# A gated retention and sparse attention block: the first stage's buffers, chunk order and queues

## The chip, the cores and the metric

The kernel runs on one core of one Trainium2 chip. The metric is the device time of one execution in microseconds; lower is better. The runs of the kernel before have a median of 1617.08 us (three runs, 1615.84 to 1619.18).

## The reference

One decoder block over 512 positions and 2048 channels, all in 32-bit floats. An adaptive norm makes h; fifteen projections of h, held in one matrix w_in, feed a retention branch and a sparse attention branch (NSA); both are gated, widened and merged, and one output projection closes the block.

```python
mod = silu(c) @ w_ada + b_ada                 # 2048 -> 3 * 2048
shift, scl, gate = split(mod, 3)
h = rmsnorm(x, g_norm) * (1 + scl) + shift
(r_q, r_k, r_v, r_g, n_q, n_kc, n_vc, n_ks, n_vs, n_kw, n_vw, n_g, n_bg, m_a, m_b) = split(h @ w_in)
y_ret = retention(rope(r_q), rope(r_k), r_v) * silu(r_g)
y_nsa = nsa(rope(n_q), n_kc, n_vc, rope(n_ks), n_vs, rope(n_kw), n_vw, sigmoid(n_bg)) * silu(n_g)
merged = sigmoid(m_a) * (y_ret @ w_up_ret) + sigmoid(m_b) * (y_nsa @ w_up_nsa)
x = x + gate * (merged @ w_out)
out = rmsnorm(x, g_final)
```

## The kernel before

Every large product is made of three matmuls with reduced-precision parts: activation and weight are split into a high part (a cast by ScalarE, `whi`, `hhi`) and a low part (a subtraction by VectorE, `wlo`, `hlo`), and TensorE adds high x high, high x low and low x high into a PSUM bank. Weights come in tiles of 128 x 1024 (512 KB). `plan` lists all of them in order of use; `load` runs ahead of use and issues the transfers on SP's queue while buffers are free; `split` makes the two parts of the next weight tile, three of them at most being held. The schedule is that of the program text: each engine executes its instructions in the order in which they are written.

The first stage makes h and, beside it, the first two groups of w_in (`g0`, the compressed keys and values; group 1, the keys `kT`). The modulation is computed in 8 chunks of 256 channels of shift and scale. A chunk is 8 tiles of w_ada. `ada_batch` takes two of them and runs 4 matmuls, four at a time on the four column quarters of the array (`pa`). After four batches `ada_rows` copies the sums out, `ada_cols` turns them into columns with small matmuls (`misc`), and VectorE and ScalarE make the high and low parts of two 128-channel tiles of h. `xn` multiplies x by the norm's scale first. Between batches TensorE works off a queue `todo` of steps of group 0 (one weight tile, one of four banks, 6 matmuls) and of group 1 (`k_step`: a tile with half the columns and four contraction tiles, 12 matmuls, in one of two banks; the sum is added to `kacc` by VectorE). A step carries the number of the batch from which it may run, and each batch lets about 12 matmuls go.

Buffers of the stage: 5 tiles (`raw`) and 2 pairs (`kv`), 9 tiles in all. The norm's sum of squares is 16 matmuls with a matrix of ones; `rstd_rows` turns it into the scale `rstd` after the second batch. The rotary tables are built one VectorE instruction per batch; the last `k_step`s rotate the keys. Then groups 2 to 20 follow in `run_group`, with `side` items (attention, retention) put in by `tick` at a `rate` for each step. Later stages that the change touches: the up-projections reload gates (`sg`) from memory on SP's queue, and the output's evacuation sums squares and scales the rows.

## Time and profile before

| | |
|---|---|
| median of the runs | 1617.08 us |
| profiled execution, its own time | 1619.62 us |
| its span | 1617.9 us |
| TensorE busy | 1588.0 us (98%) |
| VectorE, ScalarE busy | 712.6 us (44%), 489.2 us (30%) |
| bytes moved | 252.54 MB, mean 156 GB/s |

The span runs from the first to the last instruction of the profiled execution; its own time also holds what lies around it. TensorE's matmuls are pipelined, so its busy share is that of an engine with work in it, not of peak use.

### The profile page before, as it was taken

To read this page: it belongs to the slowest core of one execution; us is meant where nothing else is said; L and a number is where in the kernel's file an instruction comes from. 1 tells how busy PE (TensorE), PEld (TensorE's weight loads), DVE (VectorE), ACT (ScalarE), POOL (GpSimd) and SP (SyncE) were. 2 spreads that over 40 slices of the span, in tenths; PEclk is the share of its full clock that TensorE was granted. 3 is DMA by queue.
4 is the path that set the end of the run, shared out by engine and by line. 5 is a ranking of instruction groups with operands and counts; after the bars stand their busy time and mean duration, and the time that the engine had idled before them with its cause. 6 is when DMAs were issued, how large, how long until landed. Compare 5 with 4: busy or idle time off the path is not lost.

```text
span 1617.9 us, 18828 instructions
## 1 busy us (share of the span) xinstructions
PE 1588.0 (98%) x7502; PEld 1266.3 (78%) x7502; DVE 712.6 (44%) x1238; ACT 489.2 (30%) x719; POOL 33.9 (2%) x68
## 2 busy tenths in 40 slices
PE   7999999999999999999999999999999999999997
PEld 2566777888888888778888888888888888778886
DVE  5454533345534344542245343332221566654444
ACT  1223313234433534432333333332222222222223
POOL 2000000000000000000001000000001000010000
PEclk9999999999999999999999999999999999999999
DMA  9886354323323313213544554333335777884322
GB/s 373 325 312 222 112 172 152 105 91 106 103 72 98 105 59 98 92 59 111 172 143 134 178 179 147 122 124 124 112 112 167 271 230 236 260 297 182 104 79 105
DMA packets 88217, 252.54 MB, mean 156 GB/s; under 512 B 9248, under 2 KB 18528, under 8 KB 86976
## 3 DMA queue, kind: packets, MB, share of 16 engines
q1 hardware_dynamic: 80048, 235.71, 42.5%
q0 software_dynamic: 7504, 13.53, 2.7%
q10 hardware_dynamic: 576, 2.10, 0.3%
q8 instruction: 59, 0.97, 0.2%
q14 instruction: 30, 0.25, 0.0%
HBM read 224.03 MB, written 27.26 MB: 155 GB/s over the span
## 4 chain that ended last, share of the span: by engine, by line
PE 90%; DVE 4%; DMA 3%; ACT 2%; issue 1%; SPq 0%; ACTq 0%; DVEq 0%
PE g L414 58%; PE o L414 11%; PE u L414 6%; PE g L879 2%; PE o L719 2%; PE sc L682 2%; PE pa L324 2%; PE tp L705 1%; PE ssq L272 1%; PE phid L603 1%; DMA raw<-in_w_ada 1%; DVE wlo L262 1%; DMA raw<-in_w_un 1%; DMA raw<-in_w_ur 1%; PE o L716 1%
## 5 line engine op out<-in xcount | busy, mean ns | idle before, releaser
L262 DVE TENSOR_TENSOR wlo<-raw,whi 128x1024 fp32r<-128x1024 f32 x246 | 297.9, 1223 | 487.0 <-ACT whi L261 486.9
L414 PE MATMUL g<-hhi,whi 128*128 128x512 f32 x1088 | 438.2, 403 | 0.0
L414 PE MATMUL g<-hhi,wlo 128*128 128x512 f32 x1088 | 424.8, 390 | 1.6 <-DVE wlo L262 1.6
L414 PE MATMUL g<-hlo,whi 128*128 128x512 f32 x1088 | 424.1, 390 | 0.0
L261 ACT CAST whi<-raw 128x1024 fp32r<-128x1024 f32 x246 | 255.0, 1048 | 499.8 <-PE g L414 229.0
L414 PEld LDWEIGHTS g<-hhi,whi 128*128 128x128 f32 x1088 | 204.7, 188 | 56.2 <-issue 11.6
L414 PEld LDWEIGHTS g<-hhi,wlo 128*128 128x128 f32 x1088 | 204.5, 188 | 46.4 <-DVE wlo L262 2.5
L414 PEld LDWEIGHTS g<-hlo,whi 128*128 128x128 f32 x1088 | 204.8, 188 | 42.9 <-issue 1.4
L414 PE MATMUL g<-whi,hhi 128*128 128x512 f32 x320 | 133.8, 418 | 0.0
L414 PE MATMUL g<-wlo,hhi 128*128 128x512 f32 x320 | 124.9, 390 | 1.2 <-DVE wlo L262 1.2
L414 PE MATMUL g<-whi,hlo 128*128 128x512 f32 x320 | 125.0, 391 | 0.0
L414 PE MATMUL o<-whi,mhi 128*128 128x512 f32 x240 | 95.0, 396 | 0.0
L414 PE MATMUL o<-wlo,mhi 128*128 128x512 f32 x240 | 93.5, 390 | 0.0
L414 PE MATMUL o<-whi,mlo 128*128 128x512 f32 x240 | 93.4, 389 | 0.0
L414 PEld LDWEIGHTS g<-wlo,hhi 128*128 128x128 f32 x320 | 60.2, 188 | 16.7 <-issue 2.4
L414 PEld LDWEIGHTS g<-whi,hhi 128*128 128x128 f32 x320 | 60.1, 188 | 15.8 <-issue 3.2
L414 PEld LDWEIGHTS g<-whi,hlo 128*128 128x128 f32 x320 | 60.0, 188 | 13.0
L685 DVE CUSTOM_DVE_ANT_0 p<-sc,c_mask 128x128 f32<-128x128 f32 (+3 forms) x64 | 31.2, 488 | 85.3 <-PE sc L682 85.2
L706 ACT COPY pT<-tp 128x128 f32<-128x128 f32 (+3 forms) x64 | 27.3, 426 | 114.6 <-PE tp L705 114.4
L687 ACT ACTIVATE p<-p,sm 128x128 f32<-128x128 f32 (+3 forms) x64 | 36.1, 563 | 75.6 <-DVE sm L685 75.5
L414 PEld LDWEIGHTS o<-wlo,mhi 128*128 128x128 f32 x240 | 45.0, 188 | 10.6 <-issue 1.0
L719 PEld LDWEIGHTS o<-pT,vt 128*128 128x128 f32 x320 | 44.8, 190 | 10.9 <-issue 5.3
(238 smaller groups left out, 1699.8 us busy)
## 6 DMA issues: line engine op xcount, KB each, us to landing
raw<-in_w_in SPq DMA_DIRECT2D x176, 512.0 KB, 3.7
raw<-in_w_ada SPq DMA_DIRECT2D x32, 512.0 KB, 7.7
raw<-in_w_ada SPq DMA_DIRECT2D x16, 1024.0 KB, 8.1
raw<-in_w_gate SPq DMA_DIRECT2D x32, 512.0 KB, 4.7
raw<-in_w_o SPq DMA_DIRECT2D x32, 512.0 KB, 4.4
raw<-in_w_c SPq DMA_DIRECT2D x16, 512.0 KB, 4.1
raw<-in_w_un SPq DMA_DIRECT2D x16, 512.0 KB, 5.1
sg<-ma_d SPq DMA_DIRECT2D x32, 256.0 KB, 3.5
```

The costliest lines, as they stand in the source:

```text
L261: nc.scalar.copy(hi, r)
L262: nc.vector.tensor_tensor(lo, r, hi.bitcast(F32), op=OP.subtract)
L272: nc.tensor.matmul(ssq, ones, sq, start=kk == 0, stop=kk == NK - 1)
L324: nc.tensor.matmul(pa[j][32 * u:32 * u + 32, :], sc32[:, 4 * b + u, :], rs[u // 2][:, u % 2, :], start=b == 0, stop=b == 3)
L414: nc.tensor.matmul(self.banks[t], l, r, start=kk == 0 and n == 0, stop=kk == self.nk - 1 and n == 2)
L603: nc.tensor.matmul(hid[64 * v:64 * v + 64, :], wins[v, s][:, i, :], craw[v][:, i, :], start=s == 0 and i == 0, stop=s == 7 and i == 3)
L682: nc.tensor.matmul(b[:, :n], qT[:, h, t], res["kT"][:, 2 * br + g, :n], start=True, stop=True)
L685: nc.vector.tensor_tensor_reduce(p[:, :n], b[:, :n], mask[:, 512 - n:], -SCALE, 3.0e38, OP.add, OP.min, sm[:, 0:1])
L687: nc.scalar.activation(p[:, :n], p[:, :n], AF.Exp, bias=sm[:, 0:1], scale=-1.0, accum_out=sm[:, 1:2])
L706: nc.scalar.copy(pT[:, :n], b[:, :n])
L719: nc.tensor.matmul(o[:, r * P:(r + 1) * P], res["v"][:, m, 256 * br + P * g:256 * br + P * g + P], pT[:, m * P:(m + 1) * P], start=k == fi ...
L879: nc.tensor.matmul(b, l, r, start=u == 0 and m == 0, stop=u == 3 and m == 2)
```

## The change

- 17 weight buffers instead of 9 at the start: 5 `raw`, 4 halves of the two `kv` pairs, and 8 in two large tiles that are given up for `hhi1` and `hlo1`: large ones serve up to chunk 2, `kv` halves to the end of the stage. The look-ahead in the stage is 20 items instead of 12.
- The first chunk comes in two halves of 128 channels. Each tile is loaded in two transfers with pieces of 512 bytes; the first half's h tile is made, and the first steps of group 0 run with it alone (`us`). The weight's low part of that first tile is put behind h's.
- Chunk 1 keeps batches of two tiles; chunks 2 to 7 have two batches of four tiles (8 matmuls).
- Group 1 uses the ordinary weight tiles, two contraction tiles at a time (`k_step` of 6 matmuls, 8 rounds instead of 4). `w_half` is no longer read.
- Steps are queued when their h has been written in program order; the number of the batch is gone. `pop` lets 24 matmuls go after the first batch of a chunk, 18 after the second, 6 more ahead of the columns.
- The sum of squares is taken on ScalarE and VectorE for pairs of tiles, with 8 matmuls.
- The constants that the start does not need, and the gate weights `bgw`, are loaded on SP's queue at chunk 2 instead of POOL's at the start.
- The rotary tables and the keys' rotation are `side` items of groups 2 and 3 at a rate of 0.45.
- The reloads of `sg` go to POOL's queue. The output's row norm takes the first three quarters of its sum one round earlier, with one reduction and one multiply less at the end.

The added lines (what they replace is in the listing above; lines left out are marked):

```diff
...
+    late = []
...
+        if q is None:
+            late.append((t, t_in[name]))
+        else:
+            q.dma_start(t, t_in[name])
...
+    gn = load_const("gn", [P, NK], q=nc.gpsimd)
+    bsh = load_const("bsh", [P, NK], q=nc.gpsimd)
+    bsc = load_const("bsc", [P, NK], q=nc.gpsimd)
...
+    late.append((bgw, t_in["bgw"]))
...
+    late.append((posb, bcast(t_in["pos"], S)))
...
+    BATCH = [[2, 2, 2, 2]] * 2 + [[4, 4]] * 6
...
+        for u in range(8):
+            plan.append(("a", j, u))
+            if (j, u) == (0, 3):
+                plan.append(("w", "in", 0, 0))
+        plan += [("w", "in", g, j) for g in range(2) if j or g]
+    n_start = len(plan)
...
+    SRC = {"a": "w_ada", "in": "w_in", "c": "w_c1", "g": "w_gate", "up_r": "w_ur", "up_n": "w_un", "out": "w_o"}
...
+    w_idx = [i for i, it in enumerate(plan) if it[0] == "w"]
...
+    xw = [kvp.tile([P, 2, 1024], F32, tag="kv", name=f"xkv{a}") for a in range(2)]
+    xw += [bigt(f"xw{a}").rearrange("p a b -> p (a b)").rearrange("p (a b) -> p a b", b=1024) for a in range(2)]
+    slots = deque([("raw", None)] * RAWB + [("kv", xw[a][:, u, :]) for a in range(2) for u in range(2)]
+                  + [("big", xw[2 + a][:, u, :]) for a in range(2) for u in range(4)])
+    held = {}
...
+        while loaded[0] < min(idx + (20 if idx < n_start else 12), len(plan)):
...
+            while slots and (slots[0][0] == "big" and i >= n_big or slots[0][0] == "kv" and i >= n_start):
+                slots.popleft()
+            if not slots:
+                break
+            held[i] = slots.popleft()
+            r = held[i][1]
+            if r is None:
+                r = wp.tile([P, 1024], F32, tag="raw", bufs=RAWB, name=f"raw{i}")
+            if it[0] == "a" and it[1] == 0:
...
+                hb, n = divmod(it[2], 4)
+                for u in range(2):
+                    nc.sync.dma_start(r[:, 512 * u:512 * u + 512].rearrange("p (k c) -> p k c", k=4),
+                                      t_in["w_ada"][0, 2 * n + u].rearrange("p (k c) -> p k c", k=4)
+                                      [:, :, P * hb:P * hb + P])
...
+            raws[i] = r
...
+    n_big = plan.index(("a", 3, 0))
...
+        slots.append(held.pop(i))
...
+    def split(upto, part=None):
...
+            low = lambda hi=hi, lo=lo, r=r: nc.vector.tensor_tensor(lo, r, hi.bitcast(F32), op=OP.subtract)
+            if part is None:
+                low()
+            else:
+                part.append(low)
...
+    for a in range(4):
+        xk = [xT[a // 2][:, 4 * (a % 2) + u, :] for u in range(4)]
+        sq = [wk.tile([P, 512], F32, tag="ev", bufs=4, name=f"sq{a}{u}") for u in range(4)]
+        for u in range(3):
+            nc.scalar.activation(sq[u], xk[u], AF.Square)
+        nc.vector.tensor_tensor(sq[3], xk[3], xk[3], op=OP.mult)
+        for u in (0, 2):
+            nc.vector.tensor_tensor(sq[u], sq[u], sq[u + 1], op=OP.add)
+            nc.tensor.matmul(ssq, ones, sq[u], start=a == 0 and u == 0, stop=a == 3 and u == 2)
...
+    for t in range(NT):
+        nc.vector.scalar_tensor_tensor(rtmp[:, 1, :P], ssq[:, t * P:(t + 1) * P], 1.0, ident, op0=OP.mult,
+                                       op1=OP.mult, accum_out=st4[:, t:t + 1])
+    rstd_of(st4, st4, 1.0 / D, "rr", [P, NT])
+    for t in range(NT):
+        nc.vector.tensor_scalar(rtmp[:, 2, t * P:(t + 1) * P], ident, st4[:, t:t + 1], None, op0=OP.mult)
...
+    def xn(j, us):
...
+        for u in us:
+            kk = 2 * j + u
+            h = xT[kk // 8][:, kk % 8, :]
+            nc.vector.tensor_tensor(h, h, rstd, op=OP.mult)
...
+    h_hi = [bigt("hhi0", F32R), None]
+    h_lo = [bigt("hlo0", F32R), None]
...
+    def ada_batch(idx, j, s0, n):
...
+        load(idx + n - 1)
+        per = 2 if j else 4
+        w = 1024 // per
+        rs = [take(idx + u).rearrange("p (a b) -> p a b", a=per) for u in range(n)]
+        if s0 % (NK // per) == 0:
+            pa[j] = tbank(f"pa{j}_{s0}")
+        for u in range(per * n):
+            kk = (per * s0 + u) % NK
+            m = 32 * (kk % 4)
+            nc.tensor.matmul(pa[j][m:m + 32, :w], sc32[:, kk, :], rs[u // per][:, u % per, :],
+                             start=kk < 4, stop=kk >= NK - 4)
...
+    def ada_rows(j, w=512):
...
+        nc.scalar.copy(rows[:, :w], pa.pop(j)[:, :w])
...
+    def cols_mm(j, rows, us):
...
+        for n, q in enumerate([u + 2 * v for v in range(2) for u in us]):
+            misc_mm(pcol[:, j, q:q + 1], rows[:, n * P:(n + 1) * P], ones[:, 0:1])
...
+    def cols_h(j, us, between=None):
...
+        xn(j, us)
+        u0, n = us[0], len(us)
+        sh = wk.tile([P, 4], F32, tag="sh", bufs=2, name=f"sh{j}{u0}")
+        k0 = 2 * j + u0
+        nc.vector.tensor_tensor(sh[:, 0:n], pcol[:, j, u0:u0 + n], bsh[:, k0:k0 + n], op=OP.add)
+        nc.vector.tensor_tensor(sh[:, 2:2 + n], pcol[:, j, 2 + u0:2 + u0 + n], bsc[:, k0:k0 + n], op=OP.add)
+        nc.vector.scalar_tensor_tensor(sh[:, 2:2 + n], sh[:, 2:2 + n], 1.0, gn[:, k0:k0 + n], op0=OP.add, op1=OP.mult)
+        for u in range(n):
+            kk = k0 + u
...
+            if h_hi[a] is None:
+                h_hi[a], h_lo[a] = bigt("hhi1", F32R), bigt("hlo1", F32R)
...
+        def steps(self, items, us=None):
...
+            us = range(per) if us is None else us
+            done = us[-1] == per - 1
+            ks = [(self.kk + n * per + u, i, u) for n, i in enumerate(items) for u in us]
+            self.kk += per * len(items) if done else 0
...
+                if t == nt - 1 and done:
...
+            if plan[idx][0] != "w":
...
+        while idx < len(plan) and plan[idx][0] != "w":
...
+        for u in range(2):
+            kk = 2 * n + u
+            f = slice(u * 512 + t * P, u * 512 + t * P + P)
...
+                nc.tensor.matmul(b, l, r, start=u == 0 and m == 0, stop=u == 1 and m == 2)
+        if t == 3:
...
+        else:
...
+    def k_rope(t):
+        if t == 0:
+            res["kT"] = kvp.tile([P, 4, 512], F32, tag="kv", name="kT")
+        rope(res["kT"][:, t, :], kacc[t], cosT, sinT, 512, f"k{t}")
...
+    lim = [0]
...
+    def early_splits():
...
+        while len(splits) < 3 and w_idx[split_ptr[0]] < min(loaded[0], lim[0]):
...
+    def queue_item(i, us=None):
...
+        if it[2] == 0:
+            todo.extend((6 if us is None else 3, f) for f in g0.steps([i], us))
...
+            todo.extend((6, lambda t=t: k_step(i, it[3], t)) for t in range(4))
...
+    def pop(room):
...
+        while todo and room > 0:
+            early_splits()
+            n, f = todo.popleft()
...
+    i_w0 = plan.index(("w", "in", 0, 0))
+    load(0)
+    for b in range(2):
+        ada_batch(2 * b, 0, 2 * b, 2)
+    rows = ada_rows(0, 256)
+    part = []
+    split(0, part)
+    cols_mm(0, rows, (0,))
+    rstd_rows()
+    cols_h(0, (0,))
+    part[0]()
+    queue_item(i_w0, (0,))
+    ada_batch(5, 0, 4, 2)
+    pop(6)
+    ada_batch(7, 0, 6, 2)
+    rows = ada_rows(0, 256)
+    pop(6)
+    cols_mm(0, rows, (1,))
+    cols_h(0, (1,))
+    queue_item(i_w0, (1,))
+    queue_item(9)
+    idx = lim[0] = 10
+    for j in range(1, 8):
+        if j == 2:
+            for dst, src in late:
+                nc.sync.dma_start(dst, src)
+        s0 = 0
+        nb = len(BATCH[j])
+        for b, n in enumerate(BATCH[j]):
...
+            ada_batch(idx, j, s0, n)
+            idx += n
+            s0 += n
+            if b == nb - 1:
+                rows = ada_rows(j)
+                lim[0] = idx + 1
+            pop(6 if j == 1 else 48 // nb if b < nb - 1 else 42 // nb - 6)
+        pop(6)
+        cols_mm(j, rows, (0, 1))
+        cols_h(j, (0, 1))
+        for i in (idx, idx + 1):
+            queue_item(i)
+        idx += 2
+        lim[0] = idx
...
+    lim[0] = len(plan)
...
+        load(idx - 2)
+        early_splits()
+        todo.popleft()[1]()
...
+        if i == 7:
...
+    side.extend(rope_tables() + [lambda t=t: k_rope(t) for t in range(4)])
+    rate[0] = 0.45
...
+            flush()
...
+                nc.gpsimd.dma_start(sg, ma_d[w, 4 * j + t])
...
+    msq = cst.tile([P, NT], F32, name="msq")
+    rsm = cst.tile([P, NT], F32, name="rsm")
...
+            oc = slice(512 * j, 512 * j + 512)
+            row = xr[t // 2][:, t % 2, :]
+            xs = row[:, oc]
...
+            nc.vector.tensor_tensor(xs, xs, gfin[:, oc], op=OP.mult)
+            v, y, r = msq[:, t:t + 1], rsm[:, t:t + 1], rf[:, t:t + 1]
+            if j == 2:
...
+                nc.vector.tensor_reduce(v, acc[:, t, 0:3], axis=AX.X, op=OP.add)
+                nc.vector.tensor_scalar(v, v, 1.0 / D, EPS, op0=OP.mult, op1=OP.add)
...
+                nc.vector.scalar_tensor_tensor(v, acc[:, t, 3:4], 1.0 / D, v, op0=OP.mult, op1=OP.add)
+                nc.scalar.activation(y, v, AF.Sqrt)
+                nc.vector.reciprocal(y, y)
+                nc.vector.scalar_tensor_tensor(v, y, y, v, op0=OP.mult, op1=OP.mult)
+                nc.vector.tensor_scalar(v, v, -0.5, 1.5, op0=OP.mult, op1=OP.add)
+                nc.vector.tensor_tensor(r, y, v, op=OP.mult)
+                for n, q in enumerate((nc.sync, nc.scalar)):
...
+                        nc.scalar.activation(row[:, c], row[:, c], AF.Copy, scale=r)
...
+                        nc.vector.tensor_scalar(row[:, c], row[:, c], r, None, op0=OP.mult)
...
```

## Rows read from the trace of the kernel before

**Rows 1.** Busy PE, PEld, DVE, ACT, POOL, then granted clock, DMA share, GB/s, 20-40 us.

```profile
20.00:40.00 20.00, 14.99 (x81) 5.17 (x80) 11.69 (x35) 2.97 (x5) 0.00 (x0) 0.86 1.02 418
```

**Rows 2.** Waits of TensorE, first 182 us: total us, times, longest.

```profile
PE pa L324 <- DMA raw<-in_w_ada: 5.3, 4, 2.1
...
PE g L414 <- DVE wlo L262: 1.0, 1, 1.0
```

**Rows 3.** Waits of TensorE, 1250 us to the end.

```profile
PE u L414 <- DVE wlo L262: 0.5, 1, 0.5
PE u L414 <- ACT whi L261: 0.5, 1, 0.5
```

**Rows 4.** Chain that ended last, first stage: start us, us, what.

```profile
39.22 4.01 PE g L414 x12
...
112.27 0.79 PE misc L311 x8
...
113.06 0.99 PE pa L324 x8
...
114.06 2.94 PE g L414 x12
...
128.85 0.79 PE misc L311 x8
...
151.80 3.57 PE pbg L357 x32
...
155.37 5.67 PE g L414 x24
...
161.04 0.81 PE pgt L364 x8
```

**Rows 5.** Timeline, TensorE: start us, us, instruction, tile<-operands.

```profile
172.70 0.39 PE L414 MATMUL g<-whi,hhi 128*128 128x512 f32 x1
```

**Rows 6.** Transfers of 0-60 us in 40 slots of 1.5 us.

```profile
GB/s 0 109 322 394 425 383 405 243 344 423 401 361 419 412 426 415 418 429 415 421 429 412 421 407 418 426 407 421 426 412 415 76 0 164 336 382 407 377 391 358
```

**Rows 7.** Transfers of 838-846 us in 40 slots of 0.2 us.

```profile
GB/s 0 0 0 0 0 102 215 72 143 317 379 338 369 420 264 236 289 259 179 236 223 271 264 266 312 279 325 412 330 374 333 358 402 348 410 430 389 389 430 410
```

**Rows 8.** Timeline of the start: sum of squares, a batch, scale.

```profile
7.12 15.76 PE L272 MATMUL ssq<-sq,ones 128*128 128x512 f32 x32 [7.12 <-DVE sq L271]
...
22.81 1.92 PE L324 MATMUL pa<-raw,rtmp 128*32 128x512 f32 x16
...
26.12 1.16 PE L299 MATMUL prs<-rtmp,ones 128*128 128x128 f32 x8 [1.39 <-DVE rtmp L298]
...
27.32 0.69 DVE L300 COPY rtmp<-prs 128x512 f32<-128x512 f32 x1 [0.66 <-PE prs L299]
```

**Rows 9.** Timeline of the eighth chunk's h: columns, scale, high and low parts.

```profile
145.26 0.95 PE L311 MATMUL misc<-ones,rows 128*128 128x1 f32 x8
...
146.07 1.28 DVE L864 TENSOR_TENSOR xT<-xT,rtmp 128x512 f32<-128x512 f32 x2
...
148.30 0.62 ACT L345 CAST hhi<-xT 128x512 fp32r<-128x512 f32 x1 [5.18 <-DVE xT L344]
...
148.95 0.69 DVE L346 TENSOR_TENSOR hlo<-xT,hhi 128x512 fp32r<-128x512 f32 x1 [0.69 <-ACT hhi L345]
...
150.14 0.62 ACT L345 CAST hhi<-xT 128x512 fp32r<-128x512 f32 x1 [1.22 <-DVE xT L344]
...
150.79 0.69 DVE L346 TENSOR_TENSOR hlo<-xT,hhi 128x512 fp32r<-128x512 f32 x1 [0.69 <-ACT hhi L345]
```

**Rows 10.** Costliest groups of the page, splitting a weight tile: busy us, mean ns.

```profile
L262 DVE TENSOR_TENSOR wlo<-raw,whi 128x1024 fp32r<-128x1024 f32 x246 | 297.9, 1223 | 487.0 <-ACT whi L261 486.9
...
L261 ACT CAST whi<-raw 128x1024 fp32r<-128x1024 f32 x246 | 255.0, 1048 | 499.8 <-PE g L414 229.0
```

**Rows 11.** Timeline of the tail behind the last matmul.

```profile
1611.49 0.16 DVE L281 TENSOR_TENSOR frv<-frv,fry 128x1 f32<-128x1 f32 x1
1611.68 0.16 DVE L282 TENSOR_TENSOR frv<-frv,fry 128x1 f32<-128x1 f32 x1
```

More of the change, by code (lines that the diff above doesn't have):

```diff
@@ L243, in take @@
             load(i)
-        it = plan[i]
-        if it[0] == "a" and it[2] % 4 >= 2:
-            free["kv"] += it[2] % 2
-        else:
-            free["raw"] += 1
+        slots.append(held.pop(i))
         return raws.pop(i)
-    def split(upto):
+    def split(upto, part=None):
         while split_ptr[0] < min(upto + 1, len(w_idx)):
@@ L267, in block_kernel @@
     ssq = sbank("ssq")
-    for kk in range(NK):
-        sq = wk.tile([P, 512], F32, tag="ev", bufs=4, name=f"sq{kk}")
-        xk = xT[kk // 8][:, kk % 8, :]
-        nc.vector.tensor_tensor(sq, xk, xk, op=OP.mult)
-        nc.tensor.matmul(ssq, ones, sq, start=kk == 0, stop=kk == NK - 1)
+    for a in range(4):
[7 more added lines that the diff above has]
+            nc.tensor.matmul(ssq, ones, sq[u], start=a == 0 and u == 0, stop=a == 3 and u == 2)
     def rstd_of(dst, src, scale, tag, tmpshape, bufs=2):
@@ L314, in block_kernel @@
     pa = {}
-    def ada_batch(idx, j, b):
-        load(idx + 1)
-        rs = [take(idx + n).rearrange("p (a b) -> p a b", a=2) for n in range(2)]
-        if b == 0:
-            pa[j] = tbank(f"pa{j}")
-        for u in range(4):
-            nc.tensor.matmul(pa[j][32 * u:32 * u + 32, :], sc32[:, 4 * b + u, :], rs[u // 2][:, u % 2, :],
-                             start=b == 0, stop=b == 3)
-    def ada_rows(j):
+    def ada_batch(idx, j, s0, n):
[10 more added lines that the diff above has]
+                             start=kk < 4, stop=kk >= NK - 4)
@@ L445, in run_group @@
                 items = []
-        while idx < len(plan) and plan[idx][0] not in "wh":
+        while idx < len(plan) and plan[idx][0] != "w":
             between(idx, plan[idx])
```

122 lines of the change are left out of this document (removed).

## The prediction

> **What bounds the kernel now.** I read the busy windows first. In the first stage TensorE is the engine that counts, yet it idles 5.0 of the 20 us from 20 us on, at a mean granted clock of 0.86, that is partly at 1.2 instead of 2.4 GHz [rows 1]. The list of waits over the stage names the causes after the start: 5.3 us for pieces of the modulation weights, 1.0 us for one low part of a weight tile at the stage's end [rows 2]. Outside this stage, the waits of the up-projections and the output are two of 0.5 us [rows 3]. So an edit gains only if it removes TensorE's idle time, TensorE's own instructions, or the tail behind the last matmul. Next I read the chain that ended last: from 80 us on it is TensorE alone in a fixed rhythm, one chunk of the modulation in 128.85 - 112.27 = 16.58 us [rows 4]. The first matmul of the third group, which I call the end of the stage, begins at 172.70 us [rows 5].
>
> **What the stage can lose at its start.** A chunk brings 8 tiles of modulation weights and 2 of w_in, 5.24 MB. The transfers run at about 410 GB/s between 18 and 45 us [rows 6], so a chunk needs 12.8 us of transfer against 16.6 of TensorE. Transfers bind at the start only. More buffers help there and nowhere else, because from the fourth chunk on the new kernel has 9 buffers, as the old one.
>
> **Start, first half chunk.** By 9 us 2.45 MB have arrived (the first six slots of 1.5 us), and at 405 GB/s the rest of x lands near 13.3 us; 14 with the constants that stay [rows 6]. Then come 2.1 MB of half chunk, cut into 512-byte pieces. The trace has one transfer of that shape, the retention reload of 256 KB in 512-byte pieces: the slots from 841.0 to 843.4 us, in which it runs, give 256 GB/s on average [rows 7]. At that rate the half takes 8.2 us and lands at 22.2; at 410 GB/s it would take 5.1 and land at 19.1. I take the row, since it has the same piece size. The Trainium skill ("DMA: Bandwidth & Descriptors", Specifications) says that 512 bytes is the smallest transfer that reaches line rate; by it the half lands at 19.1. The trace disagrees: its 512-byte pieces went at 256 GB/s.
>
> The sum of squares loses half its matmuls (it lasted 15.76 us, paced by x), and ends near 18; 4.4 us later the scale's copy can start, as before (22.88 to 27.32) [rows 8]. But TensorE runs the half's batch first: 1.0 us after 22.2, then the rows' copy and two columns (0.9, an estimate from the 0.62 us of a 512-wide ScalarE instruction and the 0.95 of four columns [rows 9], each halved and with the gaps between) and 1.1 for the scale's own matmuls [rows 8]. Copy 0.7, one multiply 0.64, then offsets, product and cast 1.6 (as in [rows 9]) make the first high part of h ready at 28.2. Its low part takes 0.7, and the weight's low part, deferred behind it, 1.22 [rows 10]: 30.1. The second half lands at 22.2 + 1.3 + 8.2 = 31.7.
>
> From 30.1 the first 12 matmuls run partly at the lower clock, as those at 39 us in the old trace, before which TensorE had idled (4.01 us for 12 against 2.94 [rows 4]); with a batch between them they end at 35.4, columns at 36, the second high part at 38.4. Then 30 matmuls, 3 batches and columns (5 blocks of 1.48, 3 of 1.0, 0.8) end chunk 1 at about 50. Its successor's first four tiles land at 31.7 + 1.3 + 12.8 + 5.1 = 50.9. I take 50.8. At full rate for 512 bytes it would be 48.6, for then TensorE's chain, not the transfer, decides.
>
> **Each chunk.** Two batches of 8 matmuls replace four of 4. A double batch took 1.92 us against twice 1.0 [rows 8, 4], with 1.85 to the next start; 24 matmuls in one block take 5.67 against twice 2.94. So a chunk costs 0.79 + 2 x 1.85 + 2 x 5.67 = 15.83 us, 0.75 less than now. Against it stands a new wait. The old order put other work between a chunk's columns and the first use of its h; the new queue puts a double batch and one key step there. Count from the columns' start at 145.26 [rows 9]: the four parts of h are ready after 3.66, 4.38, 5.50 and 6.22 us (ends of the two casts and two subtractions). The first matmul that wants them comes after 0.79 + 1.85 + 1.48 = 4.12. The first part is there; the second costs 0.1, the third 0.67, the fourth 0.49. Together 1.26 us, so a chunk takes 17.1 us. VectorE works on nothing else in these 6 us, so its order cannot shorten it; behind the waiting matmuls on TensorE stands the whole next chunk. The price if the wait is covered is 0, if the 0.1 us gaps of semaphores grow, 1.6. Six chunks: 50.8 + 102.6 = 153.4.
>
> **After the last chunk** there is no batch to cover the same chain: one key step only, so the four parts cost 1.44 + 0.49 + 0.67 + 0.49 = 3.1 us. The nine remaining steps cost 12.9 with their switches of precision, the gates 3.57 + 0.81 [rows 4], the gates' bank 0.4: 20.8 with the wait. The stage ends at 174.2, or 1.5 us later than now. The 0.75 x 6 = 4.5 us of cheaper batches, the earlier start and the vanished idle are paid back by 7.6 + 3.1 us of waits for h.
>
> **What else moves.** The keys' rotation and the tables leave the stage: no TensorE time, but the 1.0 us wait for a low part at its end goes with them [rows 2]. They run beside groups three and four, covered by TensorE's own matmuls, two tiles of weights being split ahead; the rotated keys are first read after the fifth group, so they can be late there at no cost, and only a split held up behind one of the four rotations would show, about 1 us as now. Sixteen more key additions fall on VectorE, 0.69 us each like the subtractions of that size [rows 9], hidden under steps of 1.37 us (but see the third rival). The constants that go to SP stand in its queue behind the third chunk's loads and ahead of the fourth's: 0.95 MB, 2.3 us of transfer and about as much of issue. The fourth chunk's first tiles would land at 67 to 68, wanted at 67.9: nothing, up to 1 us. The gate reloads of the up stage leave SP for POOL's queue, so SP no longer waits for buffers ahead of weight loads; the two waits of 0.5 us should go, 1.0 in all [rows 3]. They are wanted a whole group later, so a slower issue costs nothing. In the tail one reduction and one multiply leave the chain, 0.19 us each from start to start [rows 11]: 0.4.
>
> **Sum:** +1.5 - 1.0 - 1.0 - 0.4 = -0.9 us. The profiled execution took 1619.62 us, 1.72 around its span of 1617.9, so it becomes 1618.7; the median of the runs is 2.5 us below that execution, and there the forecast is 1617.1 - 0.9 = 1616.2 us.
>
> **Rivals.**
> *The pieces of 512 bytes go at full rate.* For it: the reload's pieces lay far apart in memory, these lie 1 KB apart. Against: the row. The stage ends 2.2 us earlier, and the fourth chunk has margin: 1613.7 or, with the up to 1 us that this chunk could cost, a little less. This is the rule of the Trainium skill named above, taken as a mechanism here. Chance 0.13.
>
> *The wait for h is covered.* If VectorE reaches the two multiplies by the scale ahead of the last key addition's wait, or the second tile's parts come out as fast as the first's, 5 to 8 of the 10.7 us vanish: 1608 to 1611, I say 1609.7. For it: in the old trace TensorE never waited for h. Against: the order of the queue and the rows of the chain. Chance 0.23.
>
> *The two key banks become the bound (slower).* A key step is now 6 matmuls, 1.37 us, on two banks. Before the key steps stands the split of the next weight: from the batch's end a copy of 0.62, a cast of 1.05 and a subtraction of 1.22 [rows 9, 10] with 0.15 of gaps, 3.04 us until VectorE is free, the addition until 3.75, and the third step wants that bank after three steps, 0.21 + 3 x 1.37 = 4.31. Slack 0.56 us. Once the split is later than that, by a late tile or a busy ScalarE, each chunk pays the excess: 1 us in seven places gives 1623. Chance 0.18.
>
> The likeliest, at 0.46, is the sum above, with 1613 to 1619 as its own range.
>
> **Numbers.** About 0.2%, 3.2 us, is what a measurement of this kernel can tell from no change. The first rival lies at its edge on the fast side and the second beyond it, together 0.36; the third on the slow side, 0.18; within it 0.46. Leaving out a tenth on each side, the range is 1608.5 to 1621.5.
>
> **What would show it.** The third group's first matmul near 174 us (right between 171 and 177). In each chunk from the third to the seventh a stop of about 1.3 us in the steps of the first group, released by the casts and subtractions of h; some 3 us of it after the last columns. The first half's 16 loads at 220 to 290 GB/s. No stop of the key steps for VectorE. No wait of 1 us at the third group's second tile, none in the up stage. The forecast fails on the fast side if the stops for h are missing, and on the slow side if key steps wait for VectorE's additions or the fourth chunk for its tiles.

## The result and the profile after

The changed kernel takes 1625.55 us (median; 1624.05 to 1626.21), the kernel before 1616.46 us beside it on the same chip: a ratio of 1.0052, 95% interval 1.004 to 1.0065. It is slower, where the forecast was 1616.2 us with 1608.5 to 1621.5 as its range. The profiled execution took 1626.04 us, its span 1624.3, both 6.4 us more than before. The medians are 9.1 us apart: the profiled execution of the kernel before was 3.2 us above its median, that of the changed kernel 0.5, so the table below accounts for 6.4 of the 9.1.

| step, by the profiles | forecast | measured |
|---|---|---|
| end of the first stage (first matmul of the third group) | +1.5 | +4.9 (177.64 against 172.70) |
| from there to the up-projections (last gate of `mb`) | -1.0 | -1.1 |
| up-projections (from there to the first output evacuation) | -1.0 | +2.4 |
| output and tail | -0.4 | +0.2 |
| sum | -0.9 | +6.4 |

First the busy windows: the start, answering to [rows 1], 4 us in the tail of the first stage, and 5 us in the up-projections.

```profile
20.00:40.00 20.00, 14.91 (x107) 7.65 (x105) 10.10 (x34) 4.63 (x8) 0.00 (x0) 0.91 1.08 362
...
161.00:165.00 4.00, 4.00 (x11) 3.10 (x11) 2.95 (x3) 0.91 (x1) 0.00 (x0) 0.57 0.38 126
...
1403.00:1408.00 5.00, 4.47 (x14) 3.32 (x13) 4.96 (x5) 1.05 (x1) 0.00 (x0) 0.66 0.59 163
```

TensorE still idles 5 us of the 20 at the start. The two other windows are new: the granted clock, the eighth column, is 0.57 and 0.66 where it was 1.00 before. Now TensorE's waits, in the stage and from 1250 us on, answering to [rows 2, 3].

```profile
PE ssq L288 <- DVE sq L287: 12.9, 4, 8.7
PE g L453 <- ACT hhi L382: 6.4, 9, 2.1
PE g L453 <- DVE hlo L383: 2.0, 9, 0.2
PE g L453 <- DVE wlo L270: 0.6, 1, 0.6
...
PE u L453 <- ACT whi L269: 1.8, 1, 1.8
PE u L453 <- DVE wlo L270: 1.1, 2, 0.5
```

The 5.3 us of waits for modulation weights are gone. In their place stand 8.4 us for the parts of h: 3.3 in the first chunk, 3.0 in the fourth to the eighth (0.6 each) and 2.1 in the tail. This view counts only the time in which TensorE had no matmul in work. Counted by the starts of the matmuls, a chunk's stop costs 1.24 us and the tail's waits 3.1, and the forecast's 1.26 and 3.1 are to be compared with these. The waits of the up-projections, forecast to go, grew from 1.0 to 2.9 us. The last view is the timeline, at four places: the start [rows 8], the chunks [rows 9], the end of the stage [rows 5], and the up-projections.

```profile
8.71 3.78 PE L288 MATMUL ssq<-sq,ones 128*128 128x512 f32 x4 [8.71 <-DVE sq L287]
13.88 3.78 PE L288 MATMUL ssq<-sq,ones 128*128 128x512 f32 x4 [1.39 <-DVE sq L287]
19.05 1.98 PE L288 MATMUL ssq<-sq,ones 128*128 128x512 f32 x4 [1.39 <-DVE sq L287]
22.42 1.98 PE L288 MATMUL ssq<-sq,ones 128*128 128x512 f32 x4 [1.39 <-DVE sq L287]
24.33 1.93 PE L353 MATMUL pa<-raw,rtmp 128*32 128x256 f32 x32
...
52.27 1.29 DVE L326 TENSOR_TENSOR xT<-xT,rtmp 128x512 f32<-128x512 f32 x2
...
52.33 0.95 PE L336 MATMUL misc<-ones,rows 128*128 128x1 f32 x8
...
68.66 0.95 PE L336 MATMUL misc<-ones,rows 128*128 128x1 f32 x8
...
68.86 0.69 DVE L913 TENSOR_TENSOR kacc<-g,kacc 128x512 f32<-128x512 f32 x1 [0.68 <-PE g L907]
...
69.47 1.28 DVE L326 TENSOR_TENSOR xT<-xT,rtmp 128x512 f32<-128x512 f32 x2
...
74.20 0.50 PE L453 MATMUL g<-hhi,whi 128*128 128x512 f32 x1 [0.38 <-ACT hhi L382]
74.93 0.50 PE L453 MATMUL g<-hlo,whi 128*128 128x512 f32 x1 [0.22 <-DVE hlo L383]
...
85.81 0.95 PE L336 MATMUL misc<-ones,rows 128*128 128x1 f32 x8
...
158.23 0.50 PE L453 MATMUL g<-hhi,whi 128*128 128x512 f32 x1 [1.28 <-ACT hhi L382]
...
161.63 0.63 PE L453 MATMUL g<-hhi,whi 128*128 128x512 f32 x1
...
177.64 0.39 PE L453 MATMUL g<-whi,hhi 128*128 128x512 f32 x1
...
1391.71 0.53 POOL L1060 DMA_DIRECT2D ml_d<-ml  x1 [2.19 <-DVE ml L1058]
...
1392.23 2.16 POOL L1074 DMA_DIRECT2D sg<-ma_d  x4
...
1393.77 0.33 SPq L246 DMA_DIRECT2D raw<-in_w_un  x1
...
1402.63 0.50 PE L453 MATMUL u<-yhi_n,whi 128*128 128x512 f32 x1 [1.81 <-ACT whi L269]
1403.89 0.80 PE L453 MATMUL u<-yhi_n,wlo 128*128 128x512 f32 x1 [0.53 <-DVE wlo L270]
```

The sum of squares ends at 24.4 us, not near 18: its first two quarters run at 3.78 us for four instructions and the last two at 1.98 (the record of the granted clock begins at 17.7 us, at 2.4 GHz), and each quarter after the first waits 1.39 us for VectorE. The columns (`misc`) of the second chunk begin at 52.33, those of the third 16.3 us later, the others each 17.2 us behind the one before. In the fourth chunk VectorE makes a key addition (`kacc`) before it multiplies x by the scale (`xT`), and TensorE then stops twice for h; in the third it begins the multiplies with the columns, and the stops are missing. In the up-projections POOL issues the four gate reloads of the last group but one at once, behind the last of four stores, and 1.5 us before SP issues a weight tile, whose first part TensorE then awaits for 1.81 us.

### The profile page after: what moved, and what is told of

Read it like the earlier page. It is cut to its first block, busy times and chain, and to the rows that moved or that the text cites. A ratio compares the mean times of both kernels' runs of the same rounds, so it can differ in the third digit from the quotient of the medians.

```text
span 1624.3 us, 18932 instructions
## 1 busy us (share of the span) xinstructions
PE 1585.9 (98%) x7518; PEld 1267.0 (78%) x7518; DVE 721.0 (44%) x1253; ACT 495.4 (30%) x732; POOL 45.2 (3%) x89
## 4 chain that ended last, share of the span: by engine, by line
PE 92%; DVE 5%; ACT 2%; DMA 1%; issue 0%; SPq 0%; ACTq 0%; DVEq 0%
PE g L453 58%; PE o L453 11%; PE u L453 10%; PE o L758 2%; PE sc L721 2%; PE g L907 2%; PE tp L744 1%; PE pa L353 1%; PE phid L642 1%; DVE wlo L270 1%; PE ssq L288 1%; DVE hlo L383 1%; ACT hhi L382 1%; DVE xT L326 1%; PE o L755 1%; DVE xT L381 1%
## 5 line engine op out<-in xcount | busy, mean ns | idle before, releaser
L270 DVE TENSOR_TENSOR wlo<-raw,whi 128x1024 fp32r<-128x1024 f32 x240 | 290.9, 1223 | 503.8 <-ACT whi L269 503.6
L269 ACT CAST whi<-raw 128x1024 fp32r<-128x1024 f32 x240 | 248.6, 1047 | 498.3 <-PE g L453 248.9
```

The lines of the kernel that those rows point to most:

```text
L269: nc.scalar.copy(hi, r)
L270: low = lambda hi=hi, lo=lo, r=r: nc.vector.tensor_tensor(lo, r, hi.bitcast(F32), op=OP.subtract)
```

## The experiments

Times are medians; ratios are to the kernel before on the same chip, with 95% intervals.

**e1, e2: where the gate reloads are issued.** e1 is the changed kernel with them on SP again, e2 the kernel before with them on POOL.

```diff
-                nc.gpsimd.dma_start(sg, ma_d[w, 4 * j + t])
+                nc.sync.dma_start(sg, ma_d[w, 4 * j + t])
```

> The changed kernel with one line put back: the gate reloads of the up stage go through SP's queue again. Theory: on POOL's queue the four reloads of the last group but one stand behind that group's four stores, are issued together at 1392 us with the next weight tiles and slow them (7.7 us to landing against 6.0), which cost 2.3 us of waits and a stretch at the lower clock; so this kernel takes 2.5 to 3.5 us less than the changed one, about 1622.5, and the wait of 1.8 us is gone. Rival: the wait belongs to the stage's later phase or to its weights, not to the queue; then the time stays at 1625.5.

> The kernel before with one line changed: the gate reloads through POOL's queue. Theory: 2.5 to 3.5 us slower than before, about 1619.5, with a wait of about 1.8 us near 1400 us and a stretch of lower clock. Rival (the prediction's step): 1.0 us faster, 1615.5.

Measured: e1 1621.6 us, ratio 1.0029 (1.0019 to 1.0039); e2 1623.46 us, ratio 1.0034 (1.0022 to 1.0047). TensorE's waits from 1250 us on, first e1, then e2:

```profile
PE u L453 <- DVE wlo L270: 0.5, 1, 0.5
```

```profile
PE u L414 <- ACT whi L261: 1.8, 1, 1.8
PE u L414 <- DVE wlo L262: 0.5, 1, 0.5
```

The loss moves with this one line. From the last gate of `mb` to the first output evacuation it takes 215.8 us before, 218.2 after, 214.5 in e1 and 217.5 in e2. A single profile is no exact measure of it: in the fifteen profiles with the reloads on SP's queue the stretch took 213.3 to 216.2 us, in the five with them on POOL's 216.5 to 218.4. The 215.8 of the kernel before lies near the top of the first range, so 2.4 us is a low figure for this loss. In e2 the granted clock falls to 1.2 GHz at 1402.0 us for 3.4 us, in e1 nowhere in these stages. By its ratio e2 lost 5.5 us, more than the 2.5 to 3.5 expected: in its profile 1.7 us lie in this stretch and 2.3 in the first stage, which this line does not touch and where the clock fell twice more than before (at 53.8 and 81.1 us). So e2 shows the direction, and e1, with 3.7 us in the time and in the stretch, the size.

**e3, e4: the wait for h.** e3 leaves out the last pop of the second chunk, so that one step of group 1 more is queued behind every later chunk. e4 puts 8 matmuls that nobody reads ahead of the second step of the tail.

```diff
-        pop(6)
+        if j > 1:
+            pop(6)
         cols_mm(j, rows, (0, 1))
```

> The changed kernel, but chunk 1 leaves one key step more in the queue, so that from then on two key steps and a double batch stand between a chunk's columns and the first use of its h. Theory: the wait for h of 1.3 us in each of chunks 3 to 7 goes, the wait after the last chunk falls from 3.1 to 1.8 us and with it the stretch of lower clock (1.7 us); the first stage ends 8 to 9.5 us earlier, at 168 to 170 us, total about 1617. Rival 1: transfers or the key banks come next, and only 3 us are gained. Rival 2: the waits are not the loss; same time.

```diff
+        if i == 1:
+            fb = tbank("fill")
+            for n in range(8):
+                nc.tensor.matmul(fb, hhi(0)[:, :P], hhi(1), start=n == 0, stop=n == 7)
         todo.popleft()[1]()
```

> The changed kernel with 8 extra matmuls, whose result nobody reads, put into the wait for h behind the last chunk (1.8 us of work in a pause of 1.5 us and the pauses after it). Theory of the clock: the pause lowered the clock to 1.2 GHz for 3.4 us, which cost 1.7 us; with the pause filled the clock stays at 2.4 GHz, and the stage ends 1.3 to 1.7 us earlier although TensorE has more to do. Rival: the lower clock has another cause, and the time is the same or up to 0.5 us longer.

Measured: e3 1617.97 us, ratio 1.0004 (0.9995 to 1.0013); e4 1624.25 us, ratio 1.0039 (1.0025 to 1.0053). The timeline of e3, columns of two chunks and the third group:

```profile
82.35 0.95 PE L336 MATMUL misc<-ones,rows 128*128 128x1 f32 x8
...
98.24 0.95 PE L336 MATMUL misc<-ones,rows 128*128 128x1 f32 x8
...
167.85 0.39 PE L453 MATMUL g<-whi,hhi 128*128 128x512 f32 x1
```

From the fourth chunk's columns on a chunk takes 15.9 us, the 15.83 that the forecast gave it without the wait, and the stage ends 9.8 us earlier than after. Some 1.4 us of this are not the edit's: in this profile the clock rose earlier, and the sum of squares ended at 22.4 us in place of 24.4 (the second chunk's columns come 2.8 us earlier, and the step left out there is 1.4 of them). By the medians e3 gains 7.6 us. In e4 the windows of the tail show the clock whole (eighth column), at 153.4 to 160 and 160 to 164 us, where it fell in the tails of all three profiles that have these waits unfilled (after, e1 and e17):

```profile
153.40:160.00 6.60, 6.00 (x25) 4.11 (x24) 4.90 (x10) 3.14 (x4) 0.00 (x0) 1.00 0.01 3
160.00:164.00 4.00, 4.00 (x32) 1.84 (x34) 1.73 (x3) 0.00 (x0) 0.00 (x0) 1.00 0.70 184
```

With more matmuls the tail became 1.5 us shorter (columns to third group 21.6 us, 23.1 after). So the four waits there, 2.1 us in all, cost another 1.7 us: 3.4 us at half the clock. The times of e4 and after overlap; only the trace tells them apart, and it is one trace.

**e5, e8: the two edits together, and 9 buffers.** e5 has e1's and e3's edits, e8 also drops the eight buffers in the two large tiles. (The expectation of e5 names the wrong chunks for the pop; the edit is e3's.)

```diff
-    slots = deque([("raw", None)] * RAWB + [("kv", xw[a][:, u, :]) for a in range(2) for u in range(2)]
-                  + [("big", xw[2 + a][:, u, :]) for a in range(2) for u in range(4)])
+    slots = deque([("raw", None)] * RAWB + [("kv", xw[a][:, u, :]) for a in range(2) for u in range(2)])
```

> The changed kernel with both edits: the last pop of chunks 2 to 7 left out, and the gate reloads on SP's queue again. If the wait for h and the gate reloads are two separate losses, their gains add: 1625.5 - 7.6 - 3.7 = 1614 us (1612.5 to 1616), ratio to the kernel before 0.997 to 0.999, columns 15.9 us apart, the third group's first matmul at 166 to 169 us, no weight wait over 0.6 us and no fall of the clock in the up stage. Rival, that the gains share a cause (the clock of TensorE after a stop): 1617 to 1618, as with the cover alone.

> As the combined version, with 9 buffers in place of 17 (5 raw and 4 kv halves; none in the two large tiles), all else the same. Theory: the stage needs 12.8 us of transfer for a chunk of 15.9, so more than 9 buffers help at the start only: waits for modulation weights of 1 to 4 us ahead of the second chunk's columns, nothing from the fourth chunk on, 1615 to 1618 in all. Rival: the waits go on in every chunk, since 9 tiles do not hold a whole chunk of 10, and the columns lie 16.5 us or more apart: 1619 and above. Second rival: no change within 0.7 us.

Measured: e5 1614.4 us, ratio 0.9983 (0.9972 to 0.9993); e8 1617.0 us, ratio 0.9994 (0.9982 to 1.0007). The gains of e1 and e3 add. In e8 the stage ends 0.8 us later than in e5 and the columns lie 15.9 us apart from the fifth chunk on, so the theory holds there; the waits for modulation weights that it expected at the start, 1 to 4 us, are 0.8 us in all. The intervals overlap.

**e6, e17: the sum of squares.** e6 is e5 with the old sum of 16 matmuls; e17 is the changed kernel with other buffers for every second quarter of the squares.

```diff
-            nc.scalar.activation(sq[u], xk[u], AF.Square)
...
-            nc.tensor.matmul(ssq, ones, sq[u], start=a == 0 and u == 0, stop=a == 3 and u == 2)
+        nc.vector.tensor_tensor(sq, xk, xk, op=OP.mult)
+        nc.tensor.matmul(ssq, ones, sq, start=kk == 0, stop=kk == NK - 1)
```

```diff
-        sq = [wk.tile([P, 512], F32, tag="ev", bufs=4, name=f"sq{a}{u}") for u in range(4)]
+        tg = [("p", 3)] * 3 + [("rot", 1)] if a % 2 else [("ev", 4)] * 4
+        sq = [wk.tile([P, 512], F32, tag=tg[u][0], bufs=tg[u][1], name=f"sq{a}{u}") for u in range(4)]
```

> As the combined version (cover, gate reloads on SP), but the sum of squares is again 16 matmuls, each behind one square on VectorE. If the late end of the sum (24.4 us where 18 was forecast) comes from the eight matmuls running at 1.2 GHz with too little work to raise the clock, sixteen in a row end near 18 to 20 us, the rows' copy and the scale follow the landing of the half chunk (23.3), the first columns of the second chunk come 1 to 2.5 us earlier, and the time falls by the same: 1612 to 1613. Rival, that the landing of the pieces sets the start: columns within 0.7 us of the combined version's, no change.

> The changed kernel, with every second quarter of the squares in four other buffers, all else the same. If the turns of squares and matmuls on four buffers make the sum late, squares run a quarter ahead, the waits of 1.4 us go, the sum ends at 18.5 to 21 us, the first batch starts when the half chunk lands (21.5 to 22.5 in place of 24.3), the second chunk's columns come at 49.5 to 51 in place of 52.3 (48.8 to 52.3 in the traces so far that load the first chunk in halves), and the time is 1623 to 1624.5. Rival, that the low clock alone makes it late: with the matmuls at 1.2 GHz until 18 us the sum still ends at 23 or later, and nothing moves.

Measured: e6 1613.72 us, ratio 0.9974 (0.9965 to 0.9984), no gain over e5 that can be told; its sum ends at 22.8 us and its columns come 1.4 us later than e5's, so that theory falls. e17 1622.39 us, ratio 1.003 (1.0018 to 1.0043). The timeline of e17:

```profile
8.49 7.58 PE L289 MATMUL ssq<-sq,ones 128*128 128x512 f32 x12 [8.49 <-DVE sq L288]
16.30 1.98 PE L289 MATMUL ssq<-sq,ones 128*128 128x512 f32 x4 [0.22 <-DVE sq L288]
18.21 2.16 PE L354 MATMUL pa<-raw,rtmp 128*32 128x256 f32 x24
...
46.54 0.95 PE L337 MATMUL misc<-ones,rows 128*128 128x1 f32 x8
...
64.43 0.94 PE L337 MATMUL misc<-ones,rows 128*128 128x1 f32 x8
```

The sum ends at 18.3 us, where the forecast had it. The waits of 1.39 us are gone, and the second chunk's columns come 5.8 us earlier than after: 4.1 us are gained by the first half's columns, the rest where after's clock falls at 34.7 us and e17's does not. So the four buffers made it late: squares had to wait until the matmuls of the quarter before had read theirs. The low clock only stretched this, to 24.4 us, where e5, at 2.4 GHz from 12.0 us on, ended at 22.3:

```profile
13.55 1.98 PE L288 MATMUL ssq<-sq,ones 128*128 128x512 f32 x4 [1.39 <-DVE sq L287]
...
20.29 1.98 PE L288 MATMUL ssq<-sq,ones 128*128 128x512 f32 x4 [1.39 <-DVE sq L287]
```

Of the 5.8 us 2.4 are left at the end of the stage: the third chunk's columns come 4.2 us earlier than after and the fourth's 3.4, since batches now wait 2.4 us in all for tiles, and in the tail the clock is low for 6.8 us in place of 3.4. e18 and e15, below, differ by the same edit alone, with the wait for h covered: there the stage ends 3.4 us earlier (165.65 against 169.00).

**e7, e18: halves or the whole chunk.** e7 is e5 with the first chunk loaded whole (contiguous tiles of 512 KB), its two h tiles made together.

```diff
-    for b in range(2):
+    for b in range(4):
         ada_batch(2 * b, 0, 2 * b, 2)
-    rows = ada_rows(0, 256)
+    rows = ada_rows(0)
...
-    cols_mm(0, rows, (0,))
+    cols_mm(0, rows, (0, 1))
...
-            pop(6 if j == 1 else 48 // nb if b < nb - 1 else 42 // nb - 6)
+            pop((0, 12, 12, 6)[b] if j == 1 else 48 // nb if b < nb - 1 else 42 // nb - 6)
```

> As the combined version, but the first chunk is loaded whole, in contiguous tiles of 512 KB, and its two h tiles come together; the second chunk lets 0, 12, 12 and 12 matmuls go. If pieces of 512 bytes at some 290 GB/s cost the start, the whole chunk lands near 24 to 25 us (4.2 MB at 410 GB/s from 14 us), where the second half now lands near 32, and the second chunk's columns and all that follows come 2 to 5 us earlier: 1609 to 1612 us. Rival, that the halves pay because the first steps of group 0 can start at 33 us with one tile of h: columns 0 to 3 us later, 1614 to 1617.

e18 keeps the halves and has the edits of e1, e3, e15 and e17 (its text, too, names the wrong chunks for the pop).

> The changed kernel with its halves, and four mended steps: squares in eight buffers, the last pop of chunks 2 to 7 left out, gate reloads on SP's queue, late constants at chunk 4. Sum of the parts: stage end at 164.5 to 167 us, time 1611 to 1613.5. If the halves by themselves cost nothing once the sum is early, it comes within 1.5 us of e16 (the first chunk whole): 1609.8 to 1611.3; if the 512-byte pieces cost what the rates say (4.2 MB at 290 GB/s against 410 GB/s, some 4 us), it stays 2 to 4 us behind e16.

Measured: e7 1610.61 us, ratio 0.9956 (0.994 to 0.9972); e18 1612.84 us, ratio 0.997 (0.996 to 0.9981). The transfers of 0 to 60 us in slots of 1.5 us [rows 6], first e18 (halves) with a line of its timeline, then e16 (whole):

```profile
GB/s 0 109 306 387 419 429 426 426 371 305 291 290 290 327 353 292 291 290 292 362 407 415 399 415 404 410 410 410 412 410 404 415 396 412 412 407 412 412 388 412
...
64.24 0.95 PE L337 MATMUL misc<-ones,rows 128*128 128x1 f32 x8
```

```profile
GB/s 0 115 262 409 431 416 415 426 401 415 407 415 404 407 418 399 412 415 404 415 407 407 418 399 415 418 393 412 393 421 404 410 415 399 415 412 407 412 407 407
```

The 512-byte pieces run at 290 GB/s, contiguous tiles at 410. For 4.2 MB that is 4.2 us (14.5 against 10.2). The transfer engines have work all the while (the DMA share is 1.17 in e18 from 14 to 19 us, 1.02 in e16 from 14 to 24), so it is not the issue that is slow. The second chunk's columns still come alike, at 44.98 in e18 and 45.09 in e16; the third's come at 64.24 and 60.96, with 2.0 us of waits for their tiles in e18, and the stage ends 3.2 us apart. The rule of the Trainium skill ("DMA: Bandwidth & Descriptors", Specifications: line rate from 512 bytes on) does not hold for these pieces.

**e9, e10, e12 to e16: constants and the first low part.** e9 is e5 with the late constants issued on POOL's queue at the third chunk. e10 is e7 with this too, and with the first weight's low part made before the scale is copied, where VectorE waits; in e7 TensorE waited 2.2 us for that part. e12 is e10 with the old sum.

```diff
-                nc.sync.dma_start(dst, src)
+                nc.gpsimd.dma_start(dst, src)
```

```diff
+        low()
         nc.vector.tensor_copy(rstd, prs)
...
-    rstd_rows()
+    rstd_rows(part[0])
     cols_h(0, (0, 1))
-    part[0]()
```

> As the combined version of the first call (cover, gate reloads on SP), but the late constants are issued on POOL's queue at chunk 2, not on SP's. In that version the fourth chunk's batch waited 1.6 us for its tiles and its columns came 18.7 us after the third's, where the later ones came 15.9. If that is SP's queue standing behind the constants (one issue in 1.28 us from 50 to 60 us), the wait goes, all distances are 15.9 to 16.5 us, and the third group's first matmul comes 1.5 to 2.5 us earlier than 169.3, near 167. Rival, that the transfers themselves are late there (0.95 MB of constants in a stream that is still behind): the wait stays at 1 to 2 us.

> As the version with the first chunk whole, but with the late constants on POOL's queue and the first weight's low part made while VectorE waits for the scale's matmuls, not behind both low parts of h. There TensorE waited 2.2 us for that low part at 33.8 us, and the clock fell to 1.2 GHz from 36.2 us on for 3.4 us. Without the wait the first twelve matmuls run 33 to 36 us, the clock does not fall, and the stage ends 2 to 4 us earlier than 165.2: 1607 to 1609 us, ratio 0.993 to 0.995. Rival, that the second chunk's tiles are not there earlier: the wait moves to a batch, 1610 to 1611.

> The version with the first chunk whole and the weight's low part first, and the sum of squares as 16 matmuls again. In nine traces with the sum of eight matmuls TensorE reached 2.4 GHz at 11.5 to 18.2 us, in four of them at 17.0 or later, and the sum ended at 22.2 to 24.5; in the three traces read so far with 16 matmuls it rose at 10.6 to 11.1 and the sum ended at 22.7 to 22.9. If that is the cause, the sum ends near 22.8 here, the second chunk's columns come at 46.5 to 47.5 (48.5 and 47.9 in the two versions with the whole chunk), the stage ends at 163.5 to 165, and the time is 1607 to 1609.5. Rival, that it is chance, or that the second chunk's tiles set the columns: 47.9 or later, 1610 to 1611.

Measured: e9 1615.68 us (0.9986; 0.9977 to 0.9995), e10 1610.83 (0.9958; 0.9946 to 0.9971), e12 1611.1 (0.9951; 0.9938 to 0.9965): no gain in any, against the expectations. The timeline of e9 shows why:

```profile
3.53 0.56 POOL L972 DMA_DIRECT2D rtmp<-in_bgw  x1
4.09 0.53 POOL L972 DMA_DIRECT2D c_invc<-in_invc  x1
4.61 0.54 POOL L972 DMA_DIRECT2D posb<-in_pos  x1
```

POOL waits for no other engine on its way to these issues, so they go out at 3.5 to 15 us, beside x and ahead of most of the first chunk, and delay it by their 0.95 MB and more: the half chunk's last piece lands at 25.1 us (21.4 in e5), the whole chunk's last tile in e10 at 28.2 us (24.1 in e13). e13 and e14 are e10 and e12 with the constants on SP again.

> The version with the first chunk whole and the weight's low part first, with the late constants on SP's queue at chunk 2 as in the changed kernel. If the constants at the start took the gain of e10, the whole chunk lands near 24.5 us as in e7, the first twelve matmuls run without the wait of 2.2 us, and the second chunk's columns come 1.5 to 3 us before e7's 47.9 (45 to 46.4); stage end 162.5 to 164, time 1607.5 to 1609.5. Rival: the second chunk's tiles, which in e7 also came one by one at 30.9 and 32.1, set the columns, and the time stays at 1610 to 1611.

> As e13, with the sum of squares as 16 matmuls. If the sum of eight is late because TensorE is still at 1.2 GHz, this one is at least as early as e13, by up to 2 us where e13's clock rises late; if the sum is not on the path once the chunk comes whole (its landing at 24.5 is later than either end of the sum at 22.2 to 22.9), both are the same within 0.7 us.

e15 is e5, and e16 is e13, with the constants two chunks later.

```diff
-        if j == 2:
+        if j == 4:
             for dst, src in late:
                 nc.sync.dma_start(dst, src)
```

> As the combined version e5, with the late constants issued on SP's queue two chunks later (chunk 4 in place of chunk 2). If the fourth chunk's stop in e5 (columns 18.7 us behind the third's in place of 15.9) comes from ten issues standing ahead of its tiles, all distances from the third chunk on are 15.9, the stage ends near 166.5 to 167, and the time is 1612 to 1613. Rival, that the transfers themselves are behind there: the stop stays, at 1 us or more.

> As e13, with the late constants issued on SP's queue at chunk 4 in place of chunk 2. If the constants ahead of the fourth chunk's tiles made the stop, all distances between columns from the second chunk on are 15.9 to 16.3 us, the fourth chunk's columns come at 76 to 77.5, the stage ends at 161.5 to 163.5, and the time is 1607 to 1609 us, ratio 0.993 to 0.9955. Rival, that the stream of transfers is behind at the fourth chunk even without them: columns at 78.5 or later, stage end as in e13, no gain.

Measured: e13 1610.9 us (0.9956; 0.9943 to 0.9969), e14 1609.67 (0.9953; 0.994 to 0.9966), e15 1615.77 (0.9982; 0.9973 to 0.9992), e16 1609.77 (0.9946; 0.9932 to 0.9959). The timelines of e13 and of e16, columns and the fourth chunk's batch:

```profile
60.17 0.95 PE L335 MATMUL misc<-ones,rows 128*128 128x1 f32 x8
...
63.35 1.05 PE L352 MATMUL pa<-raw,rtmp 128*32 128x512 f32 x4 [1.25 <-DMA raw<-in_w_ada]
...
80.08 0.95 PE L335 MATMUL misc<-ones,rows 128*128 128x1 f32 x8
```

```profile
60.96 0.95 PE L335 MATMUL misc<-ones,rows 128*128 128x1 f32 x8
76.83 0.95 PE L335 MATMUL misc<-ones,rows 128*128 128x1 f32 x8
...
162.41 0.39 PE L452 MATMUL g<-whi,hhi 128*128 128x512 f32 x1
```

In e13 the early start is eaten by a stop at the fourth chunk, whose tiles stand behind the constants in SP's queue; two chunks later the constants cost nothing, and the stage ends at 162.41 us. e16 has the lowest ratio of all, though its interval overlaps those of e7, e10 and e12 to e14; by the trace its stage ends 10.3 us before that of the kernel before. e15 shows the stop gone as well (15.9 us), but no better time than e5: its sum ended 1.9 us later, at the low clock. e14 is no better than e13 beyond the intervals.

**e11: tables and rotation alone.** The kernel before with this one part of the change.

```diff
-    tables = deque(rope_tables())
...
-            rope(res["kT"][:, t, :], kacc[t], cosT, sinT, 512, f"k{t}")
...
+    side.extend(rope_tables() + [lambda t=t: k_rope(t) for t in range(4)])
+    rate[0] = 0.45
...
         if name == "nq0":
+            flush()
```

> The kernel before with one part of the change alone: rotary tables and the keys' rotation as side items of the third and fourth group. The forecast priced it at -1.0 us (the wait for a low part at the end of the stage goes): third group's first matmul as before at 172.7, the wait of 1.0 us behind it gone, 1615.5 to 1616. Rival, that the new wait of 1.3 us that the changed kernel shows at 335 us (scores' transposes behind a probability on VectorE) belongs to this part: 0 in sum, the wait is here too.

Measured: 1617.26 us, ratio 0.9997 (0.9988 to 1.0006). The rival holds; the timeline of e11:

```profile
330.14 0.33 PE L705 MATMUL tp<-ident,p 128*128 128x128 f32 x1 [1.26 <-DVE p L689]
```

The wait of 1.0 us at the stage's end is gone, but the attention's first transpose now waits 1.3 us, and in this trace the clock then falls for 3.4 us. (The stage ends 0.85 us earlier than before, but so do the eighth chunk's columns, ahead of this part.)

## Why the prediction was wrong

**Start (half 1, "the sum of squares ends near 18").** This step failed. It took the sum to be paced by x, and did not see that four squares and the next four share four buffers, so that VectorE and TensorE take turns. (The old sum was not paced by x either: its 15.76 us are matmuls without a stop [rows 8].) The sum ended at 24.4, the first batch began 2.6 us after the half had landed (last piece issued at 16.2, landing in 5.5 us: 21.7, near the 22.2 of the forecast), and the second chunk's columns ended at 53.1 in place of 50.8. e17 removed the turns and put the sum at 18.3.

**512-byte pieces.** Of the right kind, mis-sized: 290 GB/s, between the row's 256 and the 410 of the first rival, which did not come true. (The slots that the prediction names in [rows 7] average 262; it counted one slot early.)

**The wait for h.** Right in five chunks: 1.26 us a chunk and 17.1 us were forecast, 1.24 and 17.2 measured. The third chunk, the first of the six, took 16.3. There ScalarE copies the last key sum, and VectorE begins the multiplies at 52.27 us, as the columns begin; in the fourth chunk it first makes the last key addition and begins them 0.8 us behind the columns (69.47 against 68.66). By these two chunks the sentence that VectorE's order cannot shorten the wait does not hold: the addition, which the second rival names, is 0.8 us of it. No run moved the addition. The rival did not come true by itself; e3, which covers the wait in another way, shows what that is worth, 7.6 us of time.

**Tail after the last chunk.** Its waits came as forecast, 3.1 us by the starts. The forecast of 20.8 us fits e4, where the tail took 20.8 from the end of the columns; after, it took 22.3. What it lacked is the clock: its row of a lower clock at 39 us [rows 4] stood for the start alone, but short waits of 2.1 us in all were followed by 3.4 us at 1.2 GHz here too, worth 1.7 us.

**Third group.** The wait is gone, as forecast, and so is one of 0.5 us at 382 us; a new one of 1.3 us at 335 us, which e11 ties to this same part, was not forecast. From the stage's end to the last gate of `mb` the changed kernel's profile takes 1079.5 us and before's 1080.6, a gain near the forecast's 1.0; in the profiles where the clock falls behind the new wait it is 1081.1 and more, a loss of 0.5. That the changed kernel's own profile kept the clock is luck.

**Up-projections ("wanted a whole group later, so a slower issue costs nothing").** This step failed, by 3.4 us. It looked at when the reloads are wanted, not at what stands before them and what they meet: on POOL's queue the four of the last group but one stand behind four stores, go out together at 1392.2 us, and share the transfer engines with the weight tile issued at 1393.8, which takes 7.7 us to land in place of 6.0. TensorE waits 1.8 us, and the clock falls for 3.4 us. The Trainium skill ("DMA: Bandwidth & Descriptors", Issuing engines are not separate DMA queues) says that transfers of all issuing engines interleave on the same 16 engines; the trace agrees, with these 7.7 us. e1 and e2 show the loss on both kernels.

**Tail of the output.** The chain from the last output evacuation to the scaling of the row became 0.3 us shorter (4.39 to 4.07), but from the last matmul to the span's end it took 10.1 us after and 10.0 before. Why stays open.

**Third rival.** No key step waited for the additions after; with the wait for h covered, one did, for 0.6 us.

**Late constants.** The forecast, nothing up to 1 us, held after, since the waits for h gave the transfers time. Without these waits their price differs from profile to profile: nothing in e6, 0.6 us in e3, 1.8 in e14, 2.8 in e5 and 4.0 in e13 (distance of the fourth chunk's columns over 15.9).

## What to carry to other kernels

A transfer moved to another queue has to be followed there: it stands behind what that queue already holds, or, where the queue waits for nothing, goes out far too early, and either way it meets the loads that matter. A short stop of TensorE costs more than its length when the clock falls after it, so a wait of 1 to 2 us on the critical chain can cost 1.6 to 1.7 us more than itself, as it did in some profiles here and not in others. Where one engine fills the buffers that another empties, count the buffers before taking the slower of the two as the pace.

## What was not expected of the hardware

With the same wait of 1.3 us (at 321 to 336 us), the granted clock fell for 3.4 us in e5, e6, e8 to e13, e15 and e18 and stayed whole in after, e1, e3, e4, e7, e14, e16 and e17; e13 and e14, whose stages end alike (165.58 and 165.56 us), are 1.6 us apart at the last gate of `mb` for it. At the start the record of the clock at 2.4 GHz begins at 10.3 to 12.8 us in the six profiles with 16 matmuls in the sum, and at 11.3 to 17.9 in the fourteen with eight, in five of these at 16.5 or later; whether the fewer matmuls cause that stays open. Single profiles can so differ by 2 us without any edit, and only a timeline, not the time, tells edits of 1 us apart here.
